# Scan of a hybrid diffusion block: three decay-row buffers, one score buffer, scores copied four chunks at a time

## The chip, the cores and the metric

The kernel runs on one core of one Trainium2 chip. The metric is device time in microseconds (us) of one execution. The kernel before takes 1864.42 us, the median of three runs (1863.59 to 1870.43). Its profiled execution took 1865.5 us.

The core's engines work side by side, each through its own instructions in order: PE multiplies matrices, DVE (VectorE), ACT (ScalarE) and POOL (GpSimd) do elementwise work, and SP issues the transfers between HBM and the on-chip memory SBUF. Matrix products land in a small accumulator memory, PSUM.

## The reference, cut to what matters

One layer of a diffusion block over 1024 latent tokens and 256 context tokens. An input projection feeds three branches: a bidirectional Mamba-2 scan (SSD), a Fourier mixing and a gated MLP over positions. They are merged, projected, and followed by a feed-forward part. The change lies in the scan:

```python
def ssd_prep(xbc_raw, dt_raw, conv_w, conv_b, dt_bias):
    xbc = silu(dwconv(xbc_raw, conv_w, conv_b))          # 5-tap convolution over positions
    xs, bm, cm = split(xbc, [1024, 1280])                # 16 heads x 64; 2 groups x 128 states, twice
    dt = softplus(dt_raw + dt_bias)                      # one per position, direction and head

def ssd_scan(x, dt, a, bm, cm, init_state, with_y):      # chunks of Q = 128 positions, 8 chunks
    cum   = cumsum(dt * a)                               # per chunk
    lmat  = exp(where(tri, cum[..., :, None] - cum[..., None, :], -inf))   # decay matrix, per head
    cb    = einsum('bcqgn,bcsgn->bcgqs', cf, bf)                           # scores, per group
    y_diag = einsum('bcgqs,bgrcqs,bcsgrp->bcqgrp', cb, lmat, xf)           # inside a chunk
    y_off  = einsum('bcqgn,bcgrpn,bgrcq->bcqgrp', cf, prev, exp(cum))      # from the state before
    y = y_diag + y_off

y = ssd_scan(forward) + flip(ssd_scan(flipped inputs))
```

The scan starts from the state that the context tokens leave behind.

## The kernel before, in words

**Around the scan.** After the context tokens have been convolved, a chain over DVE, PE and SP computes their end states (`ctxm`, lines L404 to L412) and writes them to HBM as `Std`. The scan then runs for head group 0 and afterwards for head group 1, by `ssd_group(g)`. Each goes through 8 chunks forward and, in the same loop, 8 chunks backward. Beside it PE has matrix work that doesn't depend on the scan: tiles of the input projection of 48 matmuls 128x512 each, called fills here. Beside the scan of group 0 these are group 1's B tile (weights `wx9`) and C tile (`wx11`), the Fourier tiles `wf0` to `wf3` and four x tiles (`wx4` to `wx7`). Beside the scan of group 1 they are `wz0` to `wz3`, `wu0` to `wu3` and `wv0`. An x, B or C tile is followed by a convolution on DVE (L294, four instructions, and L299), an activation on ACT and transposes on PE; z and u tiles have two long DVE instructions each (L662 and L664, or L643 and L645).

**PSUM.** A fill and the score tile `pcb` (made by `ps_big`) take one of the same two PSUM buffers. A buffer comes free when its last reader is done: the copy `cbr` (L553) for `pcb`, the convolution on DVE for a fill.

**One chunk.** `cbm` (L557, DVE) is the chunk's score block, masked for the two directions. `y_off` adds what comes from the state before (transfers `ro`, exponential L505 on ACT, matmuls `po` L515, DVE L518, and L520 on POOL forward or DVE backward), and `state_step` carries the state on (POOL L525 and L530, PE L528, DVE L532). The part inside a chunk goes in two half-chunks of four heads. Each loads two rows of the decay matrix, `rf` and `rs` (L496, 256 KB each, spread over all partitions), and works:

- ACT adds a bias to `rf` per head (L568), DVE takes the minimum with `rs` per head (L569), ACT takes the exponential (L572);
- ACT writes the scores times dt into `G` (L571, forward) and into `rs` (L575, backward, over the loaded row);
- DVE adds the two (`G`, L576) and multiplies them into `rf` (L577); PE multiplies that with X (`py`, L582, four heads).

**What sets the order.** The kernel is written for a tile scheduler: the program text gives the work, priorities and pools of rotating buffers, and the scheduler orders each engine's instructions by its own forecast, in which a tile that needs a buffer waits for the last reader of the tile before. How many buffers a pool has therefore moves instructions everywhere around the scan. Pool `s3` has two buffers for a tag unless a line says otherwise, so `rf`, `rs` and `G` have two each, and `cbr` one.

## Time and profile before

| | kernel before |
|---|---|
| median of three runs | 1864.42 us |
| profiled execution, its own time | 1865.5 us |
| span of that execution | 1863.7 us |
| busy: PE / DVE / ACT / POOL | 1743.3 / 1337.7 / 896.0 / 789.9 us (94 / 72 / 48 / 42%) |
| mean granted PE clock | 0.975 |
| chain that ended last, by engine | PE 46%, DVE 9%, DMA 6% |

All times of a trace count from the start of the span. An engine's share of the whole span says little: the scan takes some 300 us of it, and what bounds it there is read from tables by stretch. A row of such a table has the stretch (start:end), its length, the busy time of PE, of PE's weight loads (PEld), of DVE, ACT and POOL with the number of instructions, the granted PE clock (1.00 is 2.4 GHz, 0.50 is 1.2 GHz), the DMA share and GB/s. A row of the timeline has start, length, engine, line, operation, tile written and tiles read, shapes, and in brackets the idle time before it and what ended that. A row of a table by lines has the count, busy time and mean ns of one, and then the idle time of the engine ahead of them with what ended it. In both, buffer numbers are left out of the names.

### The profile page before, as it was taken

How to read it: one execution, taken by the hardware profiler on the slowest of the kernel's cores; microseconds unless marked ns; L12 is line 12 of the kernel's file. 1: busy time of each engine (PE TensorE's matmuls, PEld its weight loads, DVE VectorE, ACT ScalarE, POOL GpSimd, SP SyncE). 2: the span in 40 equal slices, each digit the busy share in tenths (PEclk: the TensorE clock that was granted, in tenths of full speed). 3: DMA queues.
4: the chain of work that ended last, by engine and by line, in shares of the span. 5: the costliest groups of instructions: out<-in, count | busy, mean ns of one | idle time of the engine just before them, and what ended most of it. 6: DMA issues, size and time to landing. Idle time of an engine off the chain costs nothing.

```text
span 1863.7 us, 23811 instructions
## 1 busy us (share of the span) xinstructions
PE 1743.3 (94%) x8172; PEld 1407.8 (76%) x8172; DVE 1337.7 (72%) x1865; ACT 896.0 (48%) x1608; POOL 789.9 (42%) x534
## 2 busy tenths in 40 slices
PE   4899988999899989999899999989999999899998
PEld 3688666776678868888687888867888888677877
DVE  6876668668774665548939545889987889867686
ACT  5644366665663344444534235545555565523323
POOL 3222254316531465445545855433333433335343
PEclk9899899999999999999999999989999999999999
DMA  9212364634564325666336464133423334955742
GB/s 335 96 60 69 94 196 141 191 108 147 159 203 155 113 85 192 217 222 206 117 117 225 132 230 136 40 125 124 147 104 121 133 136 158 373 196 185 272 149 90
DMA packets 160592, 293.40 MB, mean 157 GB/s; under 512 B 17228, under 2 KB 58060, under 8 KB 159960
## 3 DMA queue, kind: packets, MB, share of 16 engines
q1 hardware_dynamic: 160472, 291.89, 47.0%
q8 instruction: 64, 1.05, 0.2%
q14 instruction: 56, 0.46, 0.1%
HBM read 221.70 MB, written 70.14 MB: 157 GB/s over the span
## 4 chain that ended last, share of the span: by engine, by line
PE 46%; DVE 9%; DMA 6%; issue 2%; ACT 1%; POOL 1%; SPq 0%; DVEq 0%; ACTq 0%; POOLq 0%
PE Yup L871 3%; PE Yup L872 3%; PE Yup L870 3%; PE Yg L870 2%; PE Yg L871 2%; PE Yg L872 2%; PE pso L154 2%; PE pso L158 2%; PE pso L156 2%; PE zup L870 1%; PE zup L871 1%; PE zup L872 1%; PE zg L870 1%; PE zg L871 1%; PE zg L872 1%
## 5 line engine op out<-in xcount | busy, mean ns | idle before, releaser
L294 DVE SCALAR_TENSOR_TENSOR acc<-psx,convw,acc 128x1023 f32<-128x1023 f32 (+1 forms) x48 | 61.3, 1277 | 24.9 <-ACT acc L290 24.7
L569 DVE SCALAR_TENSOR_TENSOR rf<-rs,ncuml,rf 128x128 f32<-128x128 f32 x128 | 54.2, 471 | 27.8 <-ACT rf L568 21.0
L1245 POOL TENSOR_TENSOR pwo<-rwo,pwo 128x512 fp32r<-128x512 f32 x32 | 47.0, 1475 | 46.5 <-ACT pwo L1244 43.0
L862 POOL TENSOR_TENSOR w1up<-A11up,w1up 128x512 fp32r<-128x512 f32 x20 | 28.6, 1432 | 79.0 <-ACT w1up L861 72.2
L1555 DVE SCALAR_TENSOR_TENSOR xf<-Yd,g,xf 128x512 f32<-128x512 f32 x64 | 46.9, 743 | 17.8 <-PE Yd L872 15.4
L862 POOL TENSOR_TENSOR w7up<-S3up,w7up 128x512 fp32r<-128x512 f32 x18 | 25.6, 1420 | 73.5 <-ACT w7up L861 40.2
L568 ACT ACTIVATE rf<-rf,ncuml 128x128 f32<-128x128 f32 x128 | 40.9, 390 | 31.3 <-DMA rf<-Rd 31.2
L158 PE MATMUL pso<-mh,pwo 128*128 128x512 f32 x128 | 50.2, 392 | 0.0
L154 PE MATMUL pso<-mh,pwo 128*128 128x512 f32 x128 | 49.8, 390 | 0.0
L156 PE MATMUL pso<-ml,pwo 128*128 128x512 f32 x128 | 49.8, 389 | 0.0
L571 ACT ACTIVATE G<-cbm,dtl 128x128 f32<-128x128 f32 x128 | 40.6, 390 | 17.5 <-DVE cbm L557 12.4
L575 ACT ACTIVATE rs<-cbm,dtl 128x128 f32<-128x128 f32 x128 | 45.1, 390 | 7.8 <-DVE rf L569 7.7
L1448 ACT ACTIVATE aa<-aa 128x512 f32<-128x512 f32 x44 | 27.7, 630 | 41.8 <-DVE aa L1429 41.5
L862 POOL TENSOR_TENSOR w4up<-A22up,w4up 128x512 fp32r<-128x512 f32 x20 | 31.8, 1591 | 31.5 <-ACT w4up L861 31.5
L530 POOL TENSOR_TENSOR st<-st,etl 128x512 f32<-128x512 f32 x24 | 32.5, 1355 | 28.6 <-DVE st L532 28.5
L582 PE MATMUL py<-rf,Xf 128*64 128x128 f32 x256 | 22.2, 298 | 20.8 <-DVE rf L577 14.6
L1493 DVE TENSOR_TENSOR gt<-gt,gp 128x1024 fp32r<-128x1024 f32 (+1 forms) x28 | 35.3, 1265 | 8.5 <-ACT gp L1492 8.5
L1450 DVE TENSOR_TENSOR gt<-gt,aa 128x512 f32<-128x512 f32 x44 | 39.7, 904 | 1.8 <-ACT aa L1448 1.7
L576 DVE TENSOR_TENSOR G<-G,rs 128x512 f32<-128x512 f32 x32 | 30.0, 937 | 14.4 <-ACT rs L575 14.3
L1492 ACT ACTIVATE gp<-gt 128x1024 fp32r<-128x1024 f32 (+1 forms) x28 | 26.6, 951 | 23.6 <-DMA Gd<-gp 12.2
L582 PEld LDWEIGHTS py<-rf,Xf 128*64 128x64 f32 x256 | 14.4, 142 | 30.6 <-DVE rf L577 17.3
L515 PEld LDWEIGHTS po<-CT,st 128*128 128x128 f32 x224 | 30.4, 198 | 8.8 <-DVE st L532 3.8
(1332 smaller groups left out, 6582.7 us busy)
## 6 DMA issues: line engine op xcount, KB each, us to landing
gh<-Gd SPq DMA_DIRECT2D x49, 256.0 KB, 5.2
gl<-Gl SPq DMA_DIRECT2D x49, 256.0 KB, 5.3
Gd<-gp SPq DMA_DIRECT2D x21, 512.0 KB, 3.1
Gl<-gt SPq DMA_DIRECT2D x21, 512.0 KB, 3.7
wm<-in_wmod_dram SPq DMA_DIRECT2D x16, 512.0 KB, 9.8
ro<-Rd SPq DMA_DIRECT2D x64, 128.0 KB, 4.1
rf<-Rd SPq DMA_DIRECT2D x32, 256.0 KB, 4.4
rs<-Rd SPq DMA_DIRECT2D x32, 256.0 KB, 3.8
```

What stands on the lines that cost most here:

```text
L154: PE.matmul(o, wh[:, k, :], xh[:, sl], start=st, stop=False)
L156: PE.matmul(o, wh[:, k, :], xl[:, sl], start=False, stop=False)
L158: last_op["mm"] = PE.matmul(o, wl[:, k, :], xh[:, sl], start=False, stop=sp)
L294: V.scalar_tensor_tensor(acc[:, lo:hi], ps[:, lo + o:hi + o], cw[:, t, j:j + 1], acc[:, lo:hi], op0=ALU.mult, op1=ALU.add)
L569: V.scalar_tensor_tensor(E[:, h, :], rs[:, h, :], ncum[:, c, 16 + f:17 + f], E[:, h, :], op0=ALU.add, op1=ALU.min)
L575: S.activation(rs[:, h, :], cbm[:, 1, :], AF.Copy, scale=dtl[:, c, f:f + 1])
L862: (V if p in on_v else G).tensor_tensor(t[:, 1, :], ap, f32(t)[:, 0, :], op=ALU.subtract)
L870: PE.matmul(o, w[:, 0, k, :], xh, start=first and k == 0, stop=False, skip_group_check=not first)
L871: PE.matmul(o, w[:, 0, k, :], xl_, start=False, stop=False, skip_group_check=not first)
L872: last_op["PE2"] = PE.matmul(o, w[:, 1, k, :], xh, start=False, stop=k == kh - 1, skip_group_check=not first)
L1245: G.tensor_tensor(t[:, 1, :], raw, f32(t)[:, 0, :], op=ALU.subtract)
L1555: V.scalar_tensor_tensor(xv, src, g2[:, dd:dd + 1], xv, op0=ALU.mult, op1=ALU.add)
```

## The change

The rows `rf` and `rs` get three buffers each, and `G` one. The scores are made and copied for four chunks at a time: `pcb` and `cbr` are allocated when chunk 0 and when chunk 4 of a group is reached, each of half the size. There is still one buffer for `cbr`, so the second half is copied once chunk 3's `cbm` has been read. The PSUM tile `pcb` is still taken from the two buffers that the fills use, now twice per group.

```diff
     def rload(c, d_, g, hg, nm, tag):
-        r = s3.tile([P, 4, P], F32, tag=tag, name=f"{nm}{g}{c}{hg}")
+        r = s3.tile([P, 4, P], F32, tag=tag, name=f"{nm}{g}{c}{hg}", bufs=3)
...
-        cbr = s3.tile([P, NCH, P], F32, tag="cbr", name=f"cbr{g}", bufs=1)
-        pcb = ps_big(f"pcb{g}")
         for c in range(NCH):
-            PE.matmul(pcb[:, c * P:(c + 1) * P], BT[:, c * P:(c + 1) * P], CT[:, c * P:(c + 1) * P],
-                      start=True, stop=True)
-        S.activation(cbr, pcb.rearrange("p (c q) -> p c q", c=NCH), AF.Copy)
-        for c in range(NCH):
+            if c % 4 == 0:
+                cbr = s3.tile([P, 4, P], F32, tag="cbr", name=f"cbr{g}{c}", bufs=1)
+                pcb = ps_big(f"pcb{g}{c}")[:, 0:512]
+                for i in range(4):
+                    cs = slice((c + i) * P, (c + i + 1) * P)
+                    PE.matmul(pcb[:, i * P:(i + 1) * P], BT[:, cs], CT[:, cs], start=True, stop=True)
+                S.activation(cbr, pcb.rearrange("p (c q) -> p c q", c=4), AF.Copy)
             X = xload(g, c, "f")
             cbm = s3.tile([P, 2, P], F32, tag="cbm", name=f"cbm{g}{c}", bufs=1)
-            V.tensor_tensor(cbm, bc(cbr[:, c, :].unsqueeze(1), [P, 2, P]), msk, op=ALU.mult)
+            V.tensor_tensor(cbm, bc(cbr[:, c % 4, :].unsqueeze(1), [P, 2, P]), msk, op=ALU.mult)
...
-                Gm = s3.tile([P, 4, P], F32, tag="G", name=f"G{g}{c}{hg}")
+                Gm = s3.tile([P, 4, P], F32, tag="G", name=f"G{g}{c}{hg}", bufs=1)
```

After L548 the lines of the kernel after have numbers higher by one for most (`py` is L583 there, `cbr` L555). From the fill `wv1` on (its first instruction follows the end of the scan of group 1) the order of instructions is the same in both.

The order moves in three places that matter below. In the rows, a number after `_` tells tiles of one name apart, and `x4` is the count of equal instructions.

PE at the start of the scan of group 0, before: `pcb_1670` is this group's score tile, `psx_2460` the fill `wx9`, `pS_1623` to `pS_1653` the context states, `psf_2536` the fill `wf0`.

```order
L551 MATMUL pcb_1670<-CT_592,BT_590 128x128 x3
L154 MATMUL psx_2460<-hh_289,wx9h 128x512 x2
L156 MATMUL psx_2460<-hl_290,wx9h 128x512 x2
...
L158 MATMUL psx_2460<-hh_548,wx9l 128x512 x2
L446 MATMUL pstx_1565<-cst,acc_1541 128x128 x4
L407 MATMUL pS_1623<-ctxm 128x512
L407 MATMUL pS_1626<-ctxm 128x512
L385 MATMUL pstc_1618<-cst,cacc_1609 128x128 x2
L407 MATMUL pS_1632<-ctxm 128x512
L407 MATMUL pS_1635<-ctxm 128x512
L154 MATMUL psf_2536<-hh_289,wf0h 128x512 x2
```

The same place after: `pcb_1670` and `pcb_2069` are the two halves of the scores, `po_1684` the scan's first y_off, `psx_2463` the fill `wx9`.

```order
L554 MATMUL pcb_2069<-CT_592,BT_590 128x128 x4
L446 MATMUL pstx_1571<-cst,acc_1541 128x128 x4
...
L407 MATMUL pS_1623<-ctxm 128x512
L407 MATMUL pS_1626<-ctxm 128x512
L385 MATMUL pstc_1618<-cst,cacc_1609 128x128 x2
L407 MATMUL pS_1635<-ctxm 128x512
...
L407 MATMUL pS_1653<-ctxm 128x512
L515 MATMUL po_1684<-CT_592,st00i 128x128 x4
L154 MATMUL psx_2463<-hh_289,wx9h 128x512 x2
```

Before, the fill `wx9` stands ahead of the context states and `wf0` among them; after, both halves of the scores stand ahead, no fill stands among the context states, and `wx9` comes behind the scan's first `po`.

PE between the two scans, before: `py_2381` belongs to the last chunk of group 0, `pcb_3150` is group 1's score tile, `psz_3972` the fill `wz0`, `pstx` the transposes of the last x tile.

```order
L158 MATMUL psx_3070<-hh_548,wx7l 128x512 x2
L551 MATMUL pcb_3150<-CT_2453,BT_2451 128x128 x5
L582 MATMUL py_2381<-rf_2382,Xf_2366 64x128 x4
L551 MATMUL pcb_3150<-CT_2453,BT_2451 128x128 x2
L446 MATMUL pstx_3051<-cst,acc_3040 128x128 x4
L582 MATMUL py_2381<-rf_2410,Xf_2366 64x128 x4
L551 MATMUL pcb_3150<-CT_2453,BT_2451 128x128
L446 MATMUL pstx_3057<-cst,acc_3040 128x128 x4
L154 MATMUL psz_3972<-hh_289,wz0h 128x512 x2
```

The same place after, where `pcb_3153` and `pcb_3552` are the two halves of group 1's scores and `psz_3978` is `wz0`.

```order
L158 MATMUL psx_3073<-hh_511,wx7l 128x512 x2
L446 MATMUL pstx_3054<-cst,acc_3043 128x128 x4
L154 MATMUL psx_3073<-hh_548,wx7h 128x512 x2
L156 MATMUL psx_3073<-hl_549,wx7h 128x512 x2
L158 MATMUL psx_3073<-hh_548,wx7l 128x512 x2
L554 MATMUL pcb_3153<-CT_2456,BT_2454 128x128 x4
L446 MATMUL pstx_3060<-cst,acc_3043 128x128 x4
L554 MATMUL pcb_3552<-CT_2456,BT_2454 128x128 x4
L154 MATMUL psz_3978<-hh_289,wz0h 128x512 x2
```

Before, the fill `wx7` ends beside the last products `py` of group 0; after, the last `py` of group 0 stands far ahead (four fills earlier, within `wx5`), and both halves of the scores stand ahead of `wz0`.

ACT in the scan of group 1, before: one chunk, whose half-chunks have the tiles `rf_3378`, `rs_3380`, `G_3382` and `rf_3406`, `rs_3408`, `G_3410`.

```order
L571 ACTIVATE G_3382<-cbm_3358,dtl 128x128 x4
L669 ACTIVATE yq_4147<-yacc_872 128x1024
L571 ACTIVATE G_3410<-cbm_3358,dtl 128x128 x4
L568 ACTIVATE rf_3378<-rf_3378,ncuml 128x128 x4
L575 ACTIVATE rs_3380<-cbm_3358,dtl 128x128 x3
L572 ACTIVATE rf_3378<-rf_3378 128x512
L575 ACTIVATE rs_3380<-cbm_3358,dtl 128x128
L568 ACTIVATE rf_3406<-rf_3406,ncuml 128x128 x4
L575 ACTIVATE rs_3408<-cbm_3358,dtl 128x128
```

The same place after, a chunk of which `rf_3580`, `rs_3582`, `G_3584` and `rf_3608`, `rs_3610`, `G_3612` are the half-chunks.

```order
L569 ACTIVATE rf_3580<-rf_3580,ncuml 128x128 x4
L670 ACTIVATE yq_4153<-yacc_872 128x1024
L505 ACTIVATE ro_3562<-ro_3562 128x512
L569 ACTIVATE rf_3608<-rf_3608,ncuml 128x128 x4
L576 ACTIVATE rs_3582<-cbm_3560,dtl 128x128 x2
L505 ACTIVATE ro_3637<-ro_3637 128x512
L572 ACTIVATE G_3584<-cbm_3560,dtl 128x128 x4
...
L576 ACTIVATE rs_3610<-cbm_3560,dtl 128x128 x3
L573 ACTIVATE rf_3608<-rf_3608 128x512
L576 ACTIVATE rs_3610<-cbm_3560,dtl 128x128
L572 ACTIVATE G_3612<-cbm_3560,dtl 128x128 x4
```

Before, `G` of both half-chunks is written ahead of the work on `rf`; after, the biases of both half-chunks come ahead, and each `G` comes late, the second one at the end of its half-chunk.

The fills that stand between the instructions of each stretch, in matmuls 128x512, counted from the two orders (a fill is 48). The scans run from the first `py` of a group to its last.

| stretch | before | after |
|---|---|---|
| `wx9` to the first `py` of group 0 | 149 | 48 |
| scan of group 0 | 331 | 242 |
| between the scans | 131 | 273 |
| scan of group 1 | 299 | 212 |
| last `py` of group 1 to the end of `wv0` | 2 | 137 |

After, three half-chunks of group 1 are multiplied (L578) before its first `py`, two before. Three convolutions (`wx9`, `wx11`, `wx4`) fall into the scan of group 0 after, four before; four z and u tiles have their DVE instructions in the scan of group 1 after, six before.

## Rows read from the trace of the kernel before

**Rows 1.** Windows: ahead of scan 0, scan 0 and scan 1.

```profile
191.00:231.00 40.00, 35.49 (x136) 24.98 (x135) 22.57 (x30) 11.62 (x17) 7.57 (x5) 0.87 0.23 74
...
246.00:387.00 141.00, 124.39 (x645) 96.41 (x647) 109.14 (x161) 94.64 (x230) 63.48 (x42) 0.95 0.56 164
...
424.00:547.00 123.00, 111.23 (x587) 83.53 (x587) 98.97 (x146) 81.05 (x204) 65.40 (x45) 0.99 0.52 152
```

**Rows 2.** Timeline: products `py` that bound the two scans.

```profile
246.18 0.66 PE L582 MATMUL py<-rf,Xf 128*64 128x128 f32 x8 [0.46 <-DVE rf L577]
...
386.42 1.12 PE L582 MATMUL py<-rf,Xf 128*64 128x128 f32 x8
...
424.01 0.65 PE L582 MATMUL py<-rf,Xf 128*64 128x128 f32 x6
...
545.77 0.66 PE L582 MATMUL py<-rf,Xf 128*64 128x128 f32 x8
```

**Rows 3.** By lines, ACT, scan 0 and then scan 1: the bias on `rf`.

```profile
L568 ACT ACTIVATE rf<-rf,ncuml 128x128 f32<-128x128 f32 x56 | 17.7, 390 | 10.9 <-DMA rf<-Rd 10.7
...
L568 ACT ACTIVATE rf<-rf,ncuml 128x128 f32<-128x128 f32 x56 | 18.1, 389 | 17.4 <-DMA rf<-Rd 17.4
```

**Rows 4.** Timeline of one buffer's cycle; waits of SP's queue in scan 1.

```profile
531.38 0.66 PE L582 MATMUL py<-rf,Xf 128*64 128x128 f32 x8
...
532.08 0.32 SPq L496 DMA_DIRECT2D rf<-Rd  x1
...
537.51 1.28 ACT L568 ACTIVATE rf<-rf,ncuml 128x128 f32<-128x128 f32 x4 [2.41 <-DMA rf<-Rd]
...
SPq L496 <- DVE G L576: 27.9, 6, 6.7
```

**Rows 5.** Timeline ahead of scan 0: fills and the context chain.

```profile
190.93 0.71 PE L154 MATMUL psx<-hh,wx9h 128*128 128x512 f32 x2
...
199.44 1.29 DVE L404 TENSOR_TENSOR ctxm<-ctxm,wdc 128x512 f32<-128x512 f32 x2 [1.87 <-ACT ctxm L388]
...
213.00 1.22 PE L154 MATMUL psf<-hh,wf0h 128*128 128x512 f32 x2 [1.98 <-DVE acc L294]
...
228.48 1.02 PE L407 MATMUL pS<-ctxm 128*128 128x512 f32 x2
...
230.27 0.69 DVE L411 TENSOR_TENSOR ctxm<-ctxm,pS 128x512 f32<-128x512 f32 x1
```

**Rows 6.** Windows of 4 us there, for the granted clock.

```profile
203.00:207.00 4.00, 2.12 (x8) 0.87 (x6) 2.98 (x4) 2.84 (x4) 1.79 (x1) 1.00 0.75 238
...
215.00:219.00 4.00, 4.00 (x13) 3.12 (x12) 0.81 (x1) 0.00 (x0) 0.09 (x1) 0.60 0.39 131
219.00:223.00 4.00, 4.00 (x18) 2.65 (x17) 1.61 (x3) 0.08 (x1) 0.96 (x1) 1.00 0.00 0
```

**Rows 7.** Windows: fills back to back; the busiest DVE stretch of a scan.

```profile
825.00:850.00 25.00, 25.00 (x112) 20.71 (x111) 15.22 (x33) 10.90 (x20) 12.59 (x10) 1.00 0.79 256
450.00:475.00 25.00, 20.68 (x107) 14.76 (x106) 22.38 (x30) 15.49 (x39) 16.33 (x12) 0.93 0.45 138
```

**Rows 8.** By lines, DVE, scan 0: the convolution after a fill.

```profile
L294 DVE SCALAR_TENSOR_TENSOR acc<-psx,convw,acc 128x1023 f32<-128x1023 f32 (+1 forms) x16 | 20.4, 1276 | 5.2 <-ACT acc L290 5.2
...
L299 DVE SCALAR_TENSOR_TENSOR acc<-tmp,acc 128x1024 f32<-128x1024 f32 x3 | 6.1, 2025 | 0.0
```

**Rows 9.** By lines, DVE, scan 1.

```profile
L569 DVE SCALAR_TENSOR_TENSOR rf<-rs,ncuml,rf 128x128 f32<-128x128 f32 x56 | 27.7, 539 | 9.7 <-ACT rf L568 9.7
L577 DVE TENSOR_TENSOR rf<-rf,G 128x512 f32<-128x512 f32 x14 | 14.2, 1013 | 0.1
...
L532 DVE TENSOR_TENSOR st<-st,pS 128x512 f32<-128x512 f32 x14 | 9.4, 678 | 6.3 <-PE pS L528 6.3
...
L643 DVE TENSOR_TENSOR x2u<-x2u,psu 128x1024 f32<-128x1024 f32 x4 | 4.9, 1213 | 1.7 <-POOL x2u L642 1.7
L645 DVE SCALAR_TENSOR_TENSOR us<-x2u,psu 128x1024 f32<-128x1024 f32 x4 | 4.8, 1208 | 0.0
```

## What we expect, and why

> **What bounds the kernel now.** I read the windows by stretch first, because the change touches only the scan and its surroundings, some 300 of 1864 us. In scan 0 and scan 1 no engine is full: PE is busy for 124.4 of 141 us and 111.2 of 123, DVE for 109.1 (77%) and 99.0 (80%) [rows 1]. So something in a chunk waits. The `py` rows bound the scans: 246.2 to 386.9 is 7.5 chunks (15 of 16 half-chunks between the first `py` and the last), 18.8 us each; 424.0 to 546.4 is 7 chunks, as two half-chunks were multiplied before the first `py`: 17.5 us each [rows 2]. The table by lines names the wait: ACT stood idle 10.7 us in scan 0 and 17.4 in scan 1 for the load of `rf` [rows 3]. The cycle of one buffer shows why: its `py` starts at 531.4, the load into it is issued at 532.1, ACT gets it at 537.5 after 2.4 us of idling, and the next `py` follows at 545.8, 14.4 us for two half-chunks even there [rows 2, 4]. SP itself waits on one queue in order, 27.9 us of it for the addition that frees `rs` [rows 4].
>
> **The change part by part.** The order of instructions is the same again from the end of fill `wv0`, so I compare that time: 546.4 plus two matmuls, 546.9 before. What is kept later on costs nothing either way. After, it is a + 7.5 r0 + b + 6.5 r1 + c: first `py` of scan 0, its chunks at r0, the work between, scan 1's chunks at r1 (6.5, since three half-chunks are multiplied ahead), the rest.
>
> Third buffers, and what a chunk costs. They let the rows of a half-chunk be asked for one half-chunk, some 7 to 9 us, earlier, more than the 5.4 us from issue to use [rows 4]. On SP these loads move ahead of `ro` and X loads of the chunk before, which queue behind them while they wait for their buffer; that is in rival 3. What comes late next is DVE. Its work per chunk after: in scan 0 109.1 less one convolution (4 x 1.28 + 2.03 = 7.1) [rows 1, 8], 102.0 / 7.5 = 13.6 us. In scan 1 99.0 less two of six z and u tiles (2 x 2.42 = 4.8), 94.2 / 7 = 13.4 [rows 1, 9]. That is the floor of r. PE's floor is near it: 242 fills at 0.223 us (25 us / 112) are 54.0 [rows 7], and its other work in scan 0 is 124.4 - 331 x 0.223 = 50.5, together 104.5 / 7.5 = 13.9; in scan 1 212 fills make 47.3 and the rest (111.2 - 299 x 0.223) / 7 x 6.5 = 41.3, 88.6 / 6.5 = 13.6. The other end is DVE's share as it is now, 77% and 80%, for a wait that only changes its name: r0 17.6, r1 16.7. Between them I take a share of 0.90: the busiest 25 us that DVE has in a scan of before are 22.4 / 25 [rows 7]. That gives r0 = 13.6 / 0.90 = 15.1 and r1 = 13.4 / 0.90 = 14.9.
>
> The single `G` buffer. ACT may write the next `G` only after DVE has read the last one in L577. In the order `G` now comes late, behind the next half-chunk's bias, so the wait on ACT has 1.6 us of other `G`-free work ahead of it and 1.6 us of L571 behind it (4 x 0.39, as L568). Queued behind it are `rs` writes and the exponential that the same half-chunk's DVE work needs. Cost: nothing where DVE has a backlog, up to the 1.6 us per half-chunk, 3.1 per chunk, where it has none. I take it into the share of 0.90 and into the range.
>
> What stays whatever the loads do: L577 reads two SBUF tiles and takes 1013 ns on average, L532, of the same shape with one input in PSUM, 678 [rows 9]. POOL's work per chunk is unchanged, so I leave the difference in. The Trainium skill (SBUF — State Buffer, Who interferes with whom) says that a DVE instruction with two SBUF inputs contends with a GpSimd instruction that reads SBUF, for an exclusively held port, and one with at most one SBUF input doesn't. The rows agree with it. By that rule the same POOL instructions in fewer microseconds would make L577 grow: POOL's 53% of scan 1 (65.4 / 123) would be 62% at 14.9 us a chunk, 0.335 us of excess 0.39, 0.1 per chunk and 1.6 us on the sum. Were the excess to go instead, the sum would be 14 x 2 x 0.335 = 9.4 us less.
>
> Start, a. Before, the context chain starts on DVE at 199.4 and ends at 231.0, among a fill's convolution and `wf0`'s matmuls [rows 5]. After, nothing of a fill stands among it. Four rounds of L404 (1.29), `pS` (1.02), L409 and L411 (0.69 each) are 3.7 us, 14.8: it ends at 214 and not 231, 17 us earlier. The price: PE has little from 195 to 213. Granted clock: after the half-idle stretch from 203 (2.12 of 4 us busy) it fell to the lower level, 1.2 GHz, and was back at 2.4 from 219 on [rows 6]. After a longer pause I expect the same at `wx9`: some 6 us at half rate (14 matmuls of 0.45), then 34 x 0.223 = 7.6, and `po` and `pS` some 2; from 213.5 this is 229. DVE needs as long: before it was 15.2 us from the chain's end to the first `py` (246.2 - 231.0), now 214 + 15.2 = 229. So a = 229 (before 246.2). If the clock stays low through all of `wx9`, a is 236; if `wx9` were hidden, DVE still gives 229.
>
> Between, b. 273 matmuls without a scan beside them are 60.9 us, where 131 were; 8 score matmuls and 32 transposes, 128x128 like the `py` (8 in 0.66 to 1.12 us [rows 2], say 0.11 each), 4.5 more. And PE waits: both halves of the scores hold PSUM, the second until chunk 3 of scan 1, so one buffer is left for the fills. `wz0` waits for the whole convolution of `wx7`, 4 x 1.28 = 5.1 [rows 8]; `wz1` for `wz0`'s two readers, put at two instructions of 1.21 [rows 9], 2.4; for `wf3` and `wx7`, which follow on buffers whose readers come late, I put half a convolution each, 2 x 2.6. Sum 12.7. Before, such waits were beside a scan. b = 60.9 + 4.5 + 12.7 = 78.1. Bounds: 65 without any wait, 84 if `wx5` and `wx6` each wait as `wz1` does.
>
> Rest, c: 137 matmuls, 30.6 us; the end of scan 1 and its two late tiles on DVE are beside it.
>
> Sum: 229 + 7.5 x 15.1 + 78.1 + 6.5 x 14.9 + 30.6 = 547.8, against 546.9: 0.9 later. What the scans win, (18.8 - 15.1) x 7.5 + (17.5 - 14.9) x 7 = 46 us, and the 17 at the start are given back because 137 - 2 = 135 matmuls come after the scan, 142 more between them, and one buffer less is there for them. With r rounded (15.05 and 14.85) it is 547.1, no change within the rounding. The profiled execution took 1865.5, 1.1 above the median of the runs; I put the same distance on the result and forecast 1864.5 + 0 = 1864.5 us. It breaks even at an average r of 15.0.
>
> **Rivals.**
> 1. The waits vanish altogether and PE bounds: r0 13.9, r1 13.6. End 229 + 104.3 + 78.1 + 88.4 + 30.6 = 530.4, 16.5 us earlier: 1848. For it: the load wait is the largest idle time that ACT has in scan 1, and the floors of DVE and PE lie together. Against it: two engines near their floors at once, in order, with neither above 91% in a scan now [rows 1].
> 2. Slower: `G`'s single buffer ties ACT to DVE. The next `G` can't be written until L577 is done, its L576 can't start until `G` and `rs` are written, so each half-chunk has a stretch in which DVE waits for ACT. DVE's share falls to 0.83, r0 16.4, r1 16.1: 229 + 123.0 + 78.1 + 104.7 + 30.6 = 565.4, 18.5 later: 1883. For it: DVE already waits on ACT now, 9.7 us ahead of L569 alone in scan 1 [rows 9], and the order puts the second `G` behind everything. Against: the DVE wait there ends with L568, which came late by the load. It decides from a share of DVE below 0.87.
> 3. The third buffers are not used: SP issues in order, and its long waits (27.9 us) [rows 4] move on to the next item. DVE's share stays at 0.77 and 0.80: 229 + 7.5 x 17.6 + 78.1 + 6.5 x 16.7 + 30.6 = 578.3, 31 later: 1896. For it: `ro` and X go through the same queue. Against: the wait that ends last is the one for `rs`, which is what has a third buffer.
>
> By the Trainium skill (DMA: Bandwidth & Descriptors, Rules for kernel authors) a transfer should be issued early and waited for late, so that its fixed cost overlaps; the 5.4 us from issue to use [rows 4] bear on it, and taken alone, with every wait for `rf` gone, it would give rival 1's 1848. ACT's idle times [rows 3] show that the overlap is missing before; no row shows the chain without it.
>
> **How the numbers follow.** Forecast, no change within its own range of 1855 to 1874: 0.36. Rival 1 and what lies between it and the forecast: 0.33. Rival 2: 0.23, rival 3: 0.08. A measurement of this kernel tells about 0.5%, 9.3 us, from no change. Rival 1 is faster by more than that, rivals 2 and 3 slower: 0.33, 0.36, 0.31. The range, 1844 to 1884, holds the forecast and both near rivals; rival 3 and an end at which b has no waits on top of rival 1 (13 us less, 1835) are left out.
>
> **What would show it.** First `py` at about 229, PE idle from 195 to 213 and `wx9` partly at the lower clock. ACT's idle time for `rf` in the scans near zero; if it stays above 10 us in each, rival 3 holds. DVE's share of a scan 0.90 and chunks of 15 us, PE under 95%; below 0.87, with DVE waiting for `G` or `rs` written by ACT, rival 2; PE above 97%, rival 1. Between the scans some 78 us, with PE waiting for DVE before `wz0` and `wz1`. Last `py` of scan 1 at about 517, `wv0` done at 547. If `wz0` and `wz1` start without waiting, b is wrong; if the part behind `wv0` takes another time than before, so is the comparison at that point.

## The result, and the profile after

The kernel after takes 1897.14 us (median of four runs, 1894.36 to 1898.28), the kernel before 1865.31 us with one more run: a ratio of 1.0153, 95% interval 1.0128 to 1.0178. It is slower: the two medians lie 31.8 us apart, and the ratio makes 28.5 us of the median before. 1897.14 lies outside the forecast's range. The profiled execution took 1894.4 us with a span of 1892.6.

The first view is the windows by stretch of the kernel after, cut at its own scans, with the columns of [rows 1].

```profile
191.00:228.00 37.00, 27.50 (x108) 17.06 (x108) 20.80 (x38) 15.20 (x34) 7.62 (x6) 0.91 0.54 151
228.00:347.00 119.00, 101.39 (x527) 75.50 (x524) 106.36 (x157) 87.06 (x229) 58.27 (x40) 0.91 0.56 169
347.00:434.00 87.00, 75.32 (x332) 60.70 (x332) 33.10 (x38) 38.03 (x65) 15.51 (x9) 0.92 0.31 95
434.00:540.00 106.00, 95.66 (x495) 69.25 (x492) 95.27 (x136) 72.63 (x191) 60.86 (x41) 0.94 0.51 149
540.00:571.00 31.00, 31.00 (x139) 25.67 (x138) 10.24 (x11) 8.29 (x8) 7.12 (x6) 1.00 0.71 259
```

The scans did get shorter: 119 us where [rows 1] have 141, and 106 where they have 123 (6.5 chunks and not 7 between the first and the last `py` there), and DVE is busy for 89 and 90% of them. The 87 us between them were 37. The products that bound the scans, in the timeline of the kernel after, answer to [rows 2]:

```profile
227.70 0.66 PE L583 MATMUL py<-rf,Xf 128*64 128x128 f32 x8 [0.91 <-DVE rf L578]
...
346.12 0.66 PE L583 MATMUL py<-rf,Xf 128*64 128x128 f32 x8
...
433.65 0.65 PE L583 MATMUL py<-rf,Xf 128*64 128x128 f32 x6
...
539.37 0.66 PE L583 MATMUL py<-rf,Xf 128*64 128x128 f32 x8 [1.08 <-DVE rf L578]
```

Fill `wv1`, from which on the order is the same, starts at 571.15, where it started at 546.94 before (its first rows, before and after):

```profile
546.94 0.63 PE L154 MATMUL psv<-hh,wv1h 128*128 128x512 f32 x2
...
571.15 0.62 PE L154 MATMUL psv<-hh,wv1h 128*128 128x512 f32 x2
```

So 24.2 of the 28.9 us by which the span grew are lost up to there. The other 4.7 come later, in the same order of instructions; the trace shows single waits there that differ by 1 to 2 us (PE for DVE's `aa`: 3.7 us at the longest, 2.1 before), and this part was not followed up.

Between the scans PE waits for a fill's PSUM buffer again and again. The timeline of PE there, the rows with idle time from 355 us on (in brackets, with what ended it):

```profile
362.22 0.84 PE L154 MATMUL psf<-hh,wf3h 128*128 128x512 f32 x2 [2.44 <-ACT fs L455]
389.38 0.73 PE L154 MATMUL psx<-hh,wx7h 128*128 128x512 f32 x2 [2.52 <-ACT fs L455]
404.43 1.16 PE L554 MATMUL pcb<-CT,BT 128*128 128x128 f32 x8 [0.45 <-ACT cbr L555]
409.42 1.22 PE L154 MATMUL psz<-hh,wz0h 128*128 128x512 f32 x2 [3.83 <-DVE acc L294]
425.50 0.73 PE L154 MATMUL psz<-hh,wz1h 128*128 128x512 f32 x2 [1.93 <-DVE th L663]
```

Of these, `wz0` waits because the second score half has the other buffer, from 404.4 us on until it is copied at 464.9. `wf3` and `wx7` wait for ACT's copy of the Fourier fill before them (L455); no score half stands in PSUM at that time, as the second one of group 0 is copied at 262.9 and the first one of group 1 is made at 402.5. Such a wait isn't new: before, `wf3` waits 2.2 us for the same copy inside scan 0, and in the experiment e10 below, which is hardly slower than the kernel before, `wf3` waits 3.8 us and `wx7` 2.9.

And each of the three longest waits costs twice. The same stretch in windows of 6 us, of which these are the ones around the three waits; the third number from the right is the granted clock:

```profile
359.00:365.00 6.00, 3.56 (x15) 2.76 (x14) 2.36 (x3) 3.07 (x3) 2.14 (x1) 0.81 0.87 257
365.00:371.00 6.00, 6.00 (x25) 4.92 (x24) 4.69 (x4) 1.72 (x3) 0.00 (x0) 0.91 0.10 28
...
389.00:395.00 6.00, 5.62 (x18) 4.45 (x19) 4.72 (x5) 2.44 (x3) 0.00 (x0) 0.72 0.35 142
...
407.00:413.00 6.00, 3.58 (x8) 2.81 (x9) 5.25 (x6) 5.88 (x18) 0.00 (x0) 0.51 0.26 77
```

With each of these pauses the clock falls towards its lower level, 1.2 GHz (0.50), and the next fill begins at half speed: PE is fully busy from 365 to 371 but does 25 matmuls, where 27 fit at the rate of [rows 7]. In the timeline, a pair of matmuls of the next fill takes 1.05 us and not 0.62 for 4 to 5 us. Around the shortest wait, 1.93 us before `wz1`, the windows show 1.00.

**A ledger for the whole stretch.** PE's work from 191 us to the start of `wv1` is nearly the same in all kernels here (length less loss is 298 to 308 us in the table behind e12), so the end of the stretch moves with what PE loses: idle time, plus length times (1 - granted clock). This is bookkeeping: it says how much PE lost, not why, and idle time at the lower clock may count in both terms. One window over the stretch, first of before and then of after:

```profile
191.00:546.94 355.94, 320.39 (x1582) 244.41 (x1581) 255.26 (x373) 220.58 (x525) 150.30 (x99) 0.95 0.51 148
```

```profile
191.00:571.15 380.15, 331.02 (x1589) 248.30 (x1587) 265.93 (x379) 221.22 (x526) 149.52 (x99) 0.93 0.50 152
```

Before: 35.6 idle + 355.9 x 0.05 = 17.8, 53.4 lost. After: 49.1 + 380.2 x 0.07 = 26.6, 75.7 lost. The difference is 22.3, the stretch is 24.2 longer. (The clock has two digits, so each of the two clock terms is good to 1.9 us.) Some 13.5 us are idle time and 9 the clock.

### The profile page after: what moved, and what is told of

Same layout as the page of the kernel before. It is cut to its first block, busy times and chain, and to the rows that moved or that the text cites. A ratio compares the mean times of both kernels' runs of the same rounds, so it can differ in the third digit from the quotient of the medians.

```text
span 1892.6 us, 23835 instructions
## 1 busy us (share of the span) xinstructions
PE 1753.0 (93%) x8172; PEld 1411.2 (75%) x8172; DVE 1344.0 (71%) x1865; ACT 897.3 (47%) x1610; POOL 791.1 (42%) x534
## 3 DMA queue, kind: packets, MB, share of 16 engines
q8 instruction: 64, 1.05, 0.2%
## 4 chain that ended last, share of the span: by engine, by line
PE 47%; DVE 7%; DMA 5%; issue 3%; ACT 1%; POOL 1%; SPq 0%; DVEq 0%; ACTq 0%; POOLq 0%
PE Yup L873 3%; PE Yup L871 3%; PE Yup L872 3%; PE Yg L871 2%; PE Yg L872 2%; PE Yg L873 2%; PE zup L871 2%; PE zup L872 2%; PE zup L873 2%; PE pso L154 2%; PE pso L158 2%; PE pso L156 2%; DMA gh<-Gd 1%; PE Yd L871 1%; PE Yd L872 1%
## 5 line engine op out<-in xcount | busy, mean ns | idle before, releaser
L294 DVE SCALAR_TENSOR_TENSOR acc<-psx,convw,acc 128x1023 f32<-128x1023 f32 (+1 forms) x48 | 61.4, 1278 | 44.7 <-ACT acc L290 44.1
L570 DVE SCALAR_TENSOR_TENSOR rf<-rs,ncuml,rf 128x128 f32<-128x128 f32 x128 | 60.3, 519 | 12.7 <-ACT rf L569 9.0
L863 POOL TENSOR_TENSOR w7up<-S3up,w7up 128x512 fp32r<-128x512 f32 x18 | 26.6, 1480 | 74.8 <-ACT w7up L862 40.9
L569 ACT ACTIVATE rf<-rf,ncuml 128x128 f32<-128x128 f32 x128 | 40.9, 389 | 25.3 <-DMA rf<-Rd 23.4
L158 PE MATMUL pso<-mh,pwo 128*128 128x512 f32 x128 | 50.2, 392 | 0.0
L576 ACT ACTIVATE rs<-cbm,dtl 128x128 f32<-128x128 f32 x128 | 44.6, 388 | 10.3 <-DVE rf L570 8.5
L520 POOL TENSOR_TENSOR yacc<-yacc,scr 128x512 f32<-128x512 f32 x16 | 23.4, 1460 | 44.5 <-DVE scr L518 35.3
L577 DVE TENSOR_TENSOR G<-G,rs 128x512 f32<-128x512 f32 x32 | 32.4, 1012 | 13.3 <-ACT rs L576 7.4
L583 PE MATMUL py<-rf,Xf 128*64 128x128 f32 x256 | 23.9, 299 | 19.4 <-DVE rf L578 11.5
L515 PE MATMUL po<-CT,st 128*128 128x128 f32 x224 | 34.4, 305 | 6.0 <-DVE st L532 6.0
L515 PEld LDWEIGHTS po<-CT,st 128*128 128x128 f32 x224 | 31.7, 213 | 10.9 <-DVE st L532 8.4
```

The lines of the kernel that those rows point to most:

```text
L158: last_op["mm"] = PE.matmul(o, wl[:, k, :], xh[:, sl], start=False, stop=sp)
L294: V.scalar_tensor_tensor(acc[:, lo:hi], ps[:, lo + o:hi + o], cw[:, t, j:j + 1], acc[:, lo:hi], op0=ALU.mult, op1=ALU.add)
L515: PE.matmul(po[:, i * P:(i + 1) * P], st[:, i * P:(i + 1) * P], CT[:, c * P:(c + 1) * P], start=True, stop=True)
L570: V.scalar_tensor_tensor(E[:, h, :], rs[:, h, :], ncum[:, c, 16 + f:17 + f], E[:, h, :], op0=ALU.add, op1=ALU.min)
L863: (V if p in on_v else G).tensor_tensor(t[:, 1, :], ap, f32(t)[:, 0, :], op=ALU.subtract)
```

## The experiments

Three theories. A: a score half in one of the fills' two PSUM buffers leaves the fills one buffer; they move out of the scans to places where PE waits, and its clock falls. B: the scan itself gives nothing back, as DVE's own work takes what the third buffers save. C: the single `G` buffer. All ratios are to the kernel before, run with the experiment, with the 95% interval.

**e1, the split alone.** `rf`, `rs` and `G` keep two buffers; against the kernel after:

```diff
-        r = s3.tile([P, 4, P], F32, tag=tag, name=f"{nm}{g}{c}{hg}", bufs=3)
+        r = s3.tile([P, 4, P], F32, tag=tag, name=f"{nm}{g}{c}{hg}")
...
-                Gm = s3.tile([P, 4, P], F32, tag="G", name=f"G{g}{c}{hg}", bufs=1)
+                Gm = s3.tile([P, 4, P], F32, tag="G", name=f"G{g}{c}{hg}")
```

> The scores in two halves (PSUM tile and copy of four chunks, each half from the two PSUM buffers of the fills) with two buffers for rf, rs and G as before. Theory A (the score halves hold the fills' PSUM buffers, so fills move out of the scans to places where PE waits and its clock falls): this part alone costs, 10 to 26 us over the kernel before (1875 to 1891): first py of group 0 near 229, 227 fill matmuls between the scans with PE idle 10 us or more there and the clock below 0.95, chunks still at 17 to 19 us. Rival B (the scan itself: DVE's work and its contention with POOL take back what the third buffers give): within 6 us of the kernel before, 1859 to 1871. Rival C (the single G buffer is the cost): the same as B.

Measured: 1.0160 (1.0118 to 1.0201), 1899.4 us. The split alone costs as much as the whole change, and three row buffers on top of it give nothing. Between its scans:

```profile
366.00:439.00 73.00, 63.40 (x275) 51.10 (x271) 28.06 (x34) 33.16 (x59) 13.31 (x7) 0.91 0.34 104
```

9.6 us idle at a clock of 0.91, where A said 10 or more and below 0.95. The size, 1899.4, is above A's range.

**e2, the single G alone.**

```diff
-                Gm = s3.tile([P, 4, P], F32, tag="G", name=f"G{g}{c}{hg}")
+                Gm = s3.tile([P, 4, P], F32, tag="G", name=f"G{g}{c}{hg}", bufs=1)
```

> The kernel before with one buffer for G instead of two and nothing else. Rival C (the single G buffer ties ACT to DVE): 10 us or more slower than the kernel before, above 1875, with ACT waiting for L577 before G more than 10 us in each scan. Theories A and B: within 6 us of the kernel before.

Measured: 0.9978 (0.9956 to 0.9999), 1864.7 us. C falls. ACT does wait for L577 before `G`, more than C's 10 us in scan 0 and less in scan 1, and the kernel is no slower for it. ACT's waits in scan 0 and in scan 1 of this kernel (total us, times, longest):

```profile
ACT G L571 <- DVE rf L577: 18.1, 10, 3.9
...
ACT G L571 <- DVE rf L577: 4.8, 4, 2.1
```

**e3, the kernel after with both halves in a small PSUM tile.**

```diff
-                pcb = ps_big(f"pcb{g}{c}")[:, 0:512]
+                pcb = ps_small(f"pcb{g}{c}", "t")
```

> The kernel after with the score halves in a small PSUM tile (the buffer of the transposes) instead of one of the two that the fills use. Theory A: at least half of the loss comes back, 1865 to 1880: PE not idle ahead of the scan of group 0, less than 6 us idle and a clock above 0.96 between the scans. Rival B: the chunks stay at 15.9 and 16.4 us and the whole within 6 us of the kernel after (1891 to 1903). Rival C: the same as B.

Measured: 1.0013 (0.9996 to 1.0030), 1874.2 us beside 1871.5 for the kernel before on that chip. Nearly the whole loss comes back from where the scores stand in PSUM. The windows ahead of scan 0, of scan 0, between and of scan 1:

```profile
191.00:257.00 66.00, 62.15 (x275) 46.98 (x273) 42.40 (x56) 26.80 (x50) 20.01 (x13) 1.00 0.52 145
257.00:372.00 115.00, 97.58 (x517) 71.85 (x519) 98.82 (x148) 86.24 (x226) 51.09 (x37) 0.94 0.60 167
372.00:426.00 54.00, 54.00 (x259) 44.06 (x255) 29.30 (x32) 28.30 (x46) 19.75 (x11) 1.00 0.37 119
426.00:538.00 112.00, 97.41 (x505) 71.92 (x505) 99.02 (x141) 77.83 (x204) 55.52 (x40) 0.92 0.52 148
```

209 fill matmuls stand between the scans and PE isn't idle there for a moment, at full clock.

**e4, the split in a small tile, without the other edits.** The diff is e1's with e3's line.

> The scores in halves as in the kernel after but in a small PSUM tile, with two buffers for rf, rs and G as before. Theory A: as the kernel before or somewhat faster by the earlier start, 1850 to 1868. Against e3 it shows what the third buffers and the single G are worth when no fill buffer is held: by rival B nothing or a loss (e3 not faster than this), by theory A e3 is faster or equal.

Measured: 1.0006 (0.9985 to 1.0026), 1873.1 us. Its scans:

```profile
258.00:390.00 132.00, 113.89 (x588) 85.29 (x585) 102.27 (x152) 90.41 (x223) 50.45 (x36) 0.92 0.54 154
...
431.00:559.00 128.00, 115.61 (x571) 86.86 (x568) 103.92 (x152) 82.91 (x214) 63.95 (x44) 0.92 0.50 150
```

Beside e3 this is the value of the third buffers (with the single `G`): scans 17 and 16 us shorter, and no difference in the time. The traces have 287 and 289 fill matmuls in the two scans here, 223 and 225 in e3.

**e5, two fill buffers taken, none held.** `cbr` keeps eight chunks.

```diff
+        for k in range(2):
+            pcb = ps_big(f"pcb{g}{k}")[:, 0:512]
...
+            S.activation(cbr[:, 4 * k:4 * k + 4, :], pcb.rearrange("p (c q) -> p c q", c=4), AF.Copy)
```

> The kernel before (two buffers for rf, rs, G, and a copy cbr of all eight chunks), but the scores made in two PSUM tiles of four chunks each from the fills' two buffers, both copied at once. Nothing is held until chunk 3. If the cost is that the second half holds a fill buffer through the first half of a scan (theory A1), this is within 8 us of the kernel before. If it is that the fills' buffers are taken twice ahead of a scan, whatever the holding (A2), 12 us or more slower than before. The order has 51, 344, 184, 304 and 29 fill matmuls in the five stretches, between the kernel before and e1 (48, 288, 227, 314, 35): A1 expects a late first fill but PE idle under 7 us between the scans.

Measured: 1.0087 (1.0054 to 1.0120), 1886.3 us. By the time A1's forecast failed and A2's came true. The trace says something else: PE was idle for 6.9 us between the scans, as A1 said, and `wv1` starts only 5.7 us later than before (e1: 29.7).

```profile
552.65 0.62 PE L154 MATMUL psv<-hh,wv1h 128*128 128x512 f32 x2
```

So up to there the loss is nearly gone once nothing is held. This profiled execution's span, 1880.6 us, is 16.9 longer than that of before; the other 11.2 come behind the start of `wv1`. Some 8 of them fall into the next 130 us, where the order isn't that of before either. Why they are lost was not followed up, so e5 doesn't show that taking a second buffer costs 0.9% of itself.

**e6, less work on POOL.** The kernel leaves out the weighting of X in the state step, so its states are other ones. The edit, on the kernel after:

```diff
...
-        G.tensor_tensor(xw, X.rearrange("p (h q) -> p h q", h=8),
-                        bc(wdl[:, c, o:o + 8].unsqueeze(2), [P, 8, 64]), op=ALU.mult)
...
-        PE.matmul(p_, Bt[:, c, :], xw.rearrange("p h q -> p (h q)"), start=True, stop=True)
+        PE.matmul(p_, Bt[:, c, :], X, start=True, stop=True)
```

> The kernel after without POOL's weighting of X in the state step (L525 left out; PE multiplies X itself), some 28 instructions of 1.2 us on POOL, two per chunk. The order is nearly that of the kernel after (48, 239, 276, 212, 137 fills). Theory D (DVE's instructions with two SBUF inputs wait for POOL, so DVE's work per chunk grows as the scan gets shorter): L577 in scan 1 falls from 1087 to below 950 ns, the cbm product from 916 to below 750, chunks are 0.5 us or more shorter, and the kernel 6 to 15 us faster than the kernel after. Rival: durations stay and the time is within 5 us of the kernel after. The start and the stretch between the scans don't change by any theory.

Measured: 1.0081 (1.0053 to 1.0109), 1885.8 us, 0.7% or some 13 us below the kernel after. By lines, DVE in scan 1, of this kernel (426 to 529 us; its lines stand three lower):

```profile
L567 DVE SCALAR_TENSOR_TENSOR rf<-rs,ncuml,rf 128x128 f32<-128x128 f32 x52 | 24.0, 504 | 4.4 <-ACT rf L566 4.4
L574 DVE TENSOR_TENSOR G<-G,rs 128x512 f32<-128x512 f32 x13 | 13.2, 1016 | 4.0 <-ACT rs L573 2.6 <-ACT G L569 1.4
L575 DVE TENSOR_TENSOR rf<-rf,G 128x512 f32<-128x512 f32 x13 | 11.6, 892 | 0.0
L529 DVE TENSOR_TENSOR st<-st,pS 128x512 f32<-128x512 f32 x14 | 9.3, 677 | 10.8 <-PE pS L525 10.8
L520 DVE TENSOR_TENSOR yacc<-yacc,scr 128x512 f32<-128x512 f32 x7 | 9.2, 1315 | 0.1
...
L555 DVE TENSOR_TENSOR cbm<-cbr,msk 128x256 f32<-128x256 f32 x6 | 4.6, 774 | 0.0
```

and the same of the kernel after (434 to 540 us):

```profile
L570 DVE SCALAR_TENSOR_TENSOR rf<-rs,ncuml,rf 128x128 f32<-128x128 f32 x52 | 26.6, 556 | 2.9 <-ACT rf L569 2.9
L577 DVE TENSOR_TENSOR G<-G,rs 128x512 f32<-128x512 f32 x13 | 14.1, 1087 | 4.5 <-ACT rs L576 2.6 <-ACT G L572 1.9
L578 DVE TENSOR_TENSOR rf<-rf,G 128x512 f32<-128x512 f32 x13 | 13.3, 1021 | 0.0
L532 DVE TENSOR_TENSOR st<-st,pS 128x512 f32<-128x512 f32 x14 | 9.3, 679 | 9.8 <-PE pS L528 9.8
...
L520 DVE TENSOR_TENSOR yacc<-yacc,scr 128x512 f32<-128x512 f32 x7 | 7.4, 1058 | 0.1
L558 DVE TENSOR_TENSOR cbm<-cbr,msk 128x256 f32<-128x256 f32 x6 | 5.5, 916 | 0.0
```

Of the five groups with two SBUF inputs four became shorter (556 to 504, 1087 to 1016, 1021 to 892 and 916 to 774 ns) and one longer (L520, 1058 to 1315); the one that reads PSUM stayed (679, 677). The five together are busy 62.6 us and not 66.9 here, and 61.7 and not 72.6 in scan 0, where again one grew (L578, 739 to 845 ns). The two bounds set for single lines were missed, the sum came: D holds for the sum of these groups and not for each of them. The Trainium skill (SBUF — State Buffer, Who interferes with whom) says that of DVE's instructions those with two SBUF inputs contend with GpSimd's reads of SBUF and those with one don't. Four of these groups and the one that reads PSUM agree; L520 doesn't, and why was not followed up. L529's idle time stayed too (10.8 us, 9.8 before), so in scan 1 the gain isn't a shorter wait for the state step.

**e7 and e8, no copy of the scores.** Each chunk's scores are made in the PSUM tile that `py` uses; e7 has three buffers for `rf` and `rs`, e8 two.

```diff
...
-            V.tensor_tensor(cbm, bc(cbr[:, c, :].unsqueeze(1), [P, 2, P]), msk, op=ALU.mult)
+            cs = slice(c * P, (c + 1) * P)
+            pcb = ps_small(f"pcb{g}{c}", "y")
+            PE.matmul(pcb[:, 0:P], BT[:, cs], CT[:, cs], start=True, stop=True)
+            V.tensor_tensor(cbm, bc(pcb[:, 0:P].unsqueeze(1), [P, 2, P]), msk, op=ALU.mult)
```

> No copy of the scores: each chunk's score block is made in the PSUM tile of py and DVE takes cbm from there; the memory freed gives three buffers for rf and rs and two for G. No fill buffer is taken. The order puts 210, 395, 49, 389 and 0 fill matmuls into the five stretches. Theory A: PE idle under 3 us ahead of scan 0 and between the scans; scans of 130 to 140 us, since 395 fills are 88 us and the scan's own PE work 50; the end of wv0 at or before 540, 5 to 15 us faster than the kernel before. Rival B (DVE's chain sets the scan, and more fills beside it only lengthen it): not faster than the kernel before.

> As e7, with two buffers for rf and rs as before: what the third row buffers are worth where no fill buffer is held. If the load of rf bounds a chunk, e7 is 8 us or more faster than this; if PE's sum of work bounds the stretch, the two are within 6 us.

Measured: e7 1.0126 (1.0105 to 1.0148), e8 1.0018 (0.9998 to 1.0038). Both forecasts for e7 by A failed, and B's, not faster than the kernel before, came true: its scans took some 159 and 154 us. Both forecasts for e8 failed too, as third buffers made e7 1% slower than e8, neither faster nor equal. DVE was at 74% from 261 to 552 us. From 261 to 560 it waited 44.7 us for ACT's bias on `rf`, and ACT 41.7 us for the load of `rf`: waits that three buffers did not take away here. Why e7 is so slow was not settled; its order packs 395 and 389 fill matmuls into the scans. It holds no fill buffer, so a loss of this size can have another cause, and theory A doesn't cover it.

**e9, a third buffer for rf with PSUM as before.** One score tile, copied whole; `rf` three buffers, `G` one.

```diff
-        r = s3.tile([P, 4, P], F32, tag=tag, name=f"{nm}{g}{c}{hg}")
+        r = s3.tile([P, 4, P], F32, tag=tag, name=f"{nm}{g}{c}{hg}", bufs=3 if nm == "rf" else 2)
...
```

> The kernel before (one score tile per group, copied whole) with three buffers for rf and one for G: what a third buffer is worth where PSUM is used as before. The order has 146, 264, 190, 211, 101 fill matmuls in the five stretches. Theory A (PE's work over the whole stretch is the same, so a faster scan only moves fills behind it): scans shorter than before by 20 us or more together, but the end of wv0 within 6 us of the kernel before and the time within 8 us of it. Rival (a chunk that waits less is time won): 15 us or more faster than the kernel before.

Measured: 1.0020 (1.0001 to 1.0039), 1876.4 us. The scans are 125 and 106 us (before 141 and 123), 33 us shorter together, and nothing is won. Theory A's account holds: 101 fill matmuls come after scan 1, and `wv1` starts at 553.0, 6 us later than before.

**e10, only the second half moved.** The kernel after, chunks 4 to 7 in the small tile.

```diff
-                pcb = ps_big(f"pcb{g}{c}")[:, 0:512]
+                pcb = ps_small(f"pcb{g}{c}", "t") if c else ps_big(f"pcb{g}{c}")[:, 0:512]
```

> The kernel after with only the second half of the scores (chunks 4 to 7) in the small PSUM tile of the transposes; the first half still takes a fill buffer. Theory A: the half that waits for chunk 3 is what costs, so the loss goes as in e3: ratio to the kernel before 1.000 to 1.006, PE busy over 90% ahead of scan 0, clock between the scans above 0.96. If taking a fill buffer at the start of a scan at all is the cost, 1.010 or more.

Measured: 1.0019 (1.0005 to 1.0034), 1876.1 us. The second half alone carries the loss: with it out of the fills' buffers, the first one costs nothing, as it did before. Between the scans the clock is 0.97 and 188 fill matmuls run at nearly full rate:

```profile
367.00:421.00 54.00, 50.70 (x239) 41.68 (x241) 29.55 (x30) 30.46 (x58) 14.02 (x7) 0.97 0.41 121
```

**e11, a candidate.** e2 with three buffers for the forward X tile:

```diff
-        X = s3.tile([P, 512], F32, tag="X" + nm, name=f"X{nm}{g}{c}", bufs=2 if nm == "f" else 1)
+        X = s3.tile([P, 512], F32, tag="X" + nm, name=f"X{nm}{g}{c}", bufs=3 if nm == "f" else 1)
```

> A candidate: the kernel before with one buffer for G and three for the forward X tile, whose late arrival holds the first products of scan 1. Expected 0.995 to 1.000 of the kernel before: as e2 (0.998), and up to 5 us less between the scans, where 120 fill matmuls stand instead of 142. Rival: no different from e2.

Measured: 1.0022 (1.0004 to 1.0040), outside the range expected and above e2. No gain.

**e12, the hold added to the kernel before.**

```diff
-        S.activation(cbr, pcb.rearrange("p (c q) -> p c q", c=NCH), AF.Copy)
+        S.activation(cbr[:, 0:4, :], pcb[:, 0:512].rearrange("p (c q) -> p c q", c=4), AF.Copy)
...
+            sc = cbr[:, c, :] if c < 4 else pcb[:, c * P:(c + 1) * P]
+            V.tensor_tensor(cbm, bc(sc.unsqueeze(1), [P, 2, P]), msk, op=ALU.mult)
```

> The suspected cost added to the kernel before, with nothing else of the change: one score tile of eight chunks, of which the first four are copied to cbr as before and the last four are read by DVE (L557) from PSUM itself, so that the tile holds one of the two fill buffers until chunk 7 instead of until the copy. Two buffers for rf, rs and G. The order has 144, 251, 168, 235 and 114 fill matmuls in the five stretches. Theory A (a fill buffer held through a scan is the cost): 1.010 or more of the kernel before, with more PE idle time and a lower mean clock from the first py of group 0 to the end of wv0. Rivals B and C (DVE's work or the single G): within 0.4% of the kernel before.

Measured: 1.0197 (1.0163 to 1.0230), 1908.6 us. One fill buffer held to chunk 7, and nothing else of the change, costs more than the change (the order moves with it, as in every kernel here). Scan 0, between, scan 1 of this kernel:

```profile
247.00:378.00 131.00, 108.16 (x545) 80.64 (x545) 106.10 (x155) 86.78 (x219) 56.12 (x39) 0.88 0.56 157
378.00:437.00 59.00, 47.97 (x206) 38.78 (x204) 22.11 (x28) 27.44 (x55) 10.90 (x6) 0.88 0.35 101
437.00:562.00 125.00, 103.73 (x522) 76.43 (x521) 94.98 (x143) 77.59 (x201) 59.95 (x41) 0.90 0.45 133
```

PE is idle for 23, 11 and 21 us and the clock is at 0.88 to 0.90 in all three, where [rows 1] have 0.95 and 0.99 in the scans.

The ledger (idle, clock loss, from 191 us to the start of `wv1`) beside the end of that stretch, for the kernels whose scan 1 ends ahead of `wv1`:

| kernel | idle us | clock | lost us | start of `wv1` | ratio |
|---|---|---|---|---|---|
| before | 35.6 | 0.95 | 53.4 | 546.9 | 1 |
| after | 49.1 | 0.93 | 75.7 | 571.2 | 1.0153 |
| e1 | 49.4 | 0.92 | 80.2 | 576.6 | 1.0160 |
| e3 | 35.9 | 0.96 | 50.2 | 548.9 | 1.0013 |
| e5 | 39.9 | 0.96 | 54.4 | 552.7 | 1.0087 |
| e6 | 43.8 | 0.95 | 62.2 | 559.7 | 1.0081 |
| e9 | 35.9 | 0.94 | 57.6 | 553.0 | 1.0020 |
| e10 | 36.1 | 0.95 | 54.2 | 553.6 | 1.0019 |
| e12 | 62.6 | 0.91 | 98.3 | 587.7 | 1.0197 |

Over a range of 40 us the end, less that of before, follows the loss within 6. Each row is one profiled execution, so a few us in it are noise, and for e1 it was the slowest of four, for e5 the fastest. The ratio is of the whole kernel: what is lost behind the start of `wv1`, most of all in e5, is not in this table.

## Why the prediction was wrong

The sum said 547.8 for the end of `wv0`; it came at 571.2. Two steps failed: the work of DVE per chunk in r0 and r1 was too small, and b priced PE's matmuls between the scans at full clock. By its own terms:

- **Start, a: right.** First `py` at 227.7 (said 229). The context chain ended at 213.6 (said 214), PE was short of work as said. One part was wrong and cost nothing: the clock fell already at 195 and was back before `wx9` came. PE in windows of 4 us:

```profile
195.00:199.00 4.00, 2.55 (x8) 1.63 (x9) 2.51 (x4) 2.58 (x5) 0.59 (x1) 0.56 0.01 2
...
203.00:207.00 4.00, 3.09 (x8) 0.97 (x6) 3.15 (x5) 0.00 (x0) 0.00 (x0) 1.00 0.43 131
```

- **Scan 0, r0: 15.9 us and not 15.1, 5.9 us on the sum.** DVE's share came at 0.894, and I took 0.90. Its work was mis-sized: 106.4 us and not 102.0. The durations of before were kept, and the largest part of what they missed is the minimum with `rs`, 29.4 us where it was 21.9 (before and after, scan 0). The cbm product (6.1 to 7.9) and L520 (6.1 to 8.7) grew too, and L578 fell from 15.7 to 11.1.

```profile
L569 DVE SCALAR_TENSOR_TENSOR rf<-rs,ncuml,rf 128x128 f32<-128x128 f32 x56 | 21.9, 438 | 14.4 <-ACT rf L568 10.1 <-DMA Xf<-Xd 4.2
...
L570 DVE SCALAR_TENSOR_TENSOR rf<-rs,ncuml,rf 128x128 f32<-128x128 f32 x61 | 29.4, 530 | 1.2 <-DMA ro<-Rd 1.1 <-ACT rf L569 0.2
```

- **Between, b: 86.9 and not 78.1, 8.8 us.** The idle time was right (11.7, said 12.7), wait by wait (2.44, 2.52, 3.83, 1.93, said 2.6, 2.6, 5.1, 2.4). What failed is the working time, 75.3 and not 65.4: the step priced 273 matmuls at the rate of an undisturbed stretch [rows 7], though it placed the waits that go with a lower clock in the same step. A clock of 0.92 over 87 us is 7 of the 9.9.
- **Scan 1, r1: 16.4 and not 14.9, 9.5 us.** The share was right again (0.899). The work per chunk was not, 14.7 and not 13.4. Part of it is a slip in the step: it divided a scan of 7 chunks by 7 and multiplied by 6.5, but only the 14 half-chunks become 13, and the y_off, state and score work of 7 chunks stays. One half-chunk less is 4.0 us (L569 and L577 of [rows 9] and L576 of the same table, below, 55.8 / 14), so the work is 94.2 - 4.0 = 90.2, not 94.2 x 6.5 / 7 = 87.5. The other part, 5.1 us, is mostly longer instructions: the sum into `G` takes 1087 ns and took 990, the cbm product 916 and 697, L520 1058 and 888. e6 shows that POOL has a hand in it. The prediction put 1.6 us on that and left it out of the sum.

```profile
L576 DVE TENSOR_TENSOR G<-G,rs 128x512 f32<-128x512 f32 x14 | 13.9, 990 | 7.4 <-ACT rs L575 7.4
```

- **Rest, c: right**, 31.1 and 30.6.

Together -1.3 + 5.9 + 8.8 + 9.5 + 0.5 = 23.4, from 547.8 to 571.2. The 4.7 us after `wv1` were not foreseen: the equal order did not take quite an equal time.

By the sum, 15.4 of the 23.4 us are chunks that took longer than forecast. The experiments show that this is not what makes the kernel slow: the scans of e3 last 115 and 112 us, those of the kernel after 119 and 106, together as long, and e3 loses 0.1%. There the rest of PE's work ran at full clock without a pause between the scans. What the sum had no term for is that a score half in a fill's buffer costs PE time ahead of the scan and in it as well: from 191 us to the end of scan 0 PE is idle for 27.1 us in the kernel after and 27.8 in e1, where a score half waits in such a buffer, and for 21.4 before, 21.3 in e3 and 21.6 in e10, where none does.

The rivals: rival 3's time, 1896, came true, but not its mechanism. It wanted unused third buffers and DVE at 0.77 and 0.80; the share rose to 0.89 and 0.90 and the scans got shorter. SP's wait for the addition that frees `rs` fell only in scan 1, from 27.9 us [rows 4] to 8.7; in scan 0 it stayed, over more and shorter waits. Scan 0 before and after, then scan 1 after:

```profile
SPq L496 <- DVE G L576: 21.3, 7, 6.8
...
SPq L496 <- DVE G L577: 21.2, 9, 3.7
...
SPq L496 <- DVE G L577: 8.7, 3, 5.8
```

ACT's idle time for `rf`, by lines in scan 0 and in scan 1 of the kernel after, against 10.9 and 17.4 in [rows 3]:

```profile
L569 ACT ACTIVATE rf<-rf,ncuml 128x128 f32<-128x128 f32 x64 | 20.5, 389 | 5.9 <-DMA rf<-Rd 4.0 <-PE py L583 1.5 <-PE po L515 0.3
...
L569 ACT ACTIVATE rf<-rf,ncuml 128x128 f32<-128x128 f32 x52 | 16.6, 389 | 17.7 <-DMA rf<-Rd 17.7
```

In scan 0 it fell to 4.0. In scan 1 it didn't fall, but 10.9 of it is one wait at the scan's start, in ACT's timeline:

```profile
439.47 1.28 ACT L569 ACTIVATE rf<-rf,ncuml 128x128 f32<-128x128 f32 x4 [10.94 <-DMA rf<-Rd]
```

Rival 2's mechanism, the single `G`, is refuted by e2, and by e1, which has two and is as slow. None of the rivals was what happened: the second score half in a fill's PSUM buffer stood in the prediction only inside b, with waits of a few us. e1, e3 and e10 show that it makes all of the loss but 0.1 to 0.2%, e12 that a held buffer alone does as much. What stays open is how much of it is the held buffer itself and how much the order that the scheduler makes of it, as every edit moves the order (e7 against e8: 1% by third buffers alone). What the third buffers win in the scans (e4 to e3: 33 us) is not time, since PE's work only moves; the prediction saw that and counted it.

## What to carry to other kernels

Where one engine has nearly constant work over a stretch, forecast the stretch by what that engine loses (idle time and time at the lower clock) and not by the speed of the chain beside it. A tile that is asked for early and read late costs the buffers that it is taken from: see who else rotates through them, and give it another home; here one line was worth 1.4%. And when a wait is put into PE's stream, the work behind it has to be priced at the clock that the trace grants after a wait of that length (here 2.4 to 3.8 us).

## What the runs showed that was not expected

- The single `G` buffer, with 22.9 us of ACT waiting for it in both scans, costs nothing; the kernel with it alone is at 0.9978 (0.9956 to 0.9999), the only one that measures below the kernel before, and barely.
- Removing 28 instructions of POOL, 1.2 us each, made four of five groups of DVE's two-input instructions 7 to 16% shorter in scan 1, the fifth 24% longer, and the kernel 13 us faster.
- Waits of PE of 2.4 to 3.8 us were followed by 4 to 5 us in which matmuls took 1.05 us a pair and not 0.62 (granted clock 0.51 to 0.91 in windows of 6 us around them).
